# Order of transposes and values in the hand-ordered prompt attention of a hybrid decoder step

## The chip, the cores and the metric

One Trainium2 chip, one core. The metric is the device time of one execution in microseconds (us); the kernel before was run three times, and the median is 2159.5 us.

## The reference, cut to what matters

The reference is one layer of a hybrid decoder for 1024 prompt tokens and 32 sample tokens: an input projection, a gated MLP mixer, an attention with three branches, a merge, and a squared-ReLU MLP. The change touches only the attention of the prompt. There are 8 query heads of width 64 in 2 key/value groups, and for every block of 128 queries and every head three softmaxes are taken, weighted by gates and added:

```
p_c = masked_softmax(einsum(qn, kc) * scale, m_c)      # compressed keys, 64 rows
o_c = einsum(p_c, vc)
p_s = masked_softmax(einsum(qr, k_s) * scale, m_s)     # selected blocks; for 1024 tokens: all causal keys
o_s = einsum(p_s, v_s)
p_w = masked_softmax(einsum(qr, k_w) * scale, m_w)     # sliding window of 512 keys
o_w = einsum(p_w, v_w)
o   = g0 * o_c + g1 * o_s + g2 * o_w
```

## The kernel before, in words

The work runs in stages on one core: projections of the first columns, their values and queries, then the attention of the prompt, the attention of the sample tokens, the merge, and the MLP. All matrix products are made of float32 halves (a rounded part and a rest), so most products come as two or three matmuls.

**The attention of the prompt** (lines 687 to 1046). A unit is one block of 128 queries and one pair of heads; there are 8 times 4 = 32 units (`pairs`, line 689). The keys of a unit, for both heads and all three branches, are laid out as runs of 128 columns, four runs to a chunk (line 722); a unit has 2 to 7 chunks, 160 chunks in all. One step of the stage handles one chunk. What is issued for a chunk c of unit u:

- **Queries**, once a unit: `q_trans` (line 698) takes a PSUM bank "PT" (there are 2), transposes four 128x128 pieces on TensorE, copies them on ScalarE (the rounded half) and subtracts on VectorE (the rest) into `QT` (2 buffers), and then calls `q_load` (line 691), which issues the two DMAs of the queries two units on, on the SP queue, into `qdl` (2 buffers).
- **Logits**: `step(c)` (line 805) takes a PSUM bank "S" (3 of them) and a buffer `P` (8), multiplies `QT` with `KT` (and `KTC` for the compressed keys), takes the masked maximum on VectorE (lines 777 and 779), and, when the last chunk of a head's branch is there, the exponentials on ScalarE (line 788). A bank S is free once its exponentials are taken. When the window branch of a head is complete, `fin` (line 791) forms the factor gate / sum on VectorE, and `scale` (line 802) multiplies the P of both branches with it on POOL.
- **Transposes**: `T(c)` (line 843) transposes the P of the chunk into a bank "PT" (line 849), copies it on ScalarE and subtracts on VectorE, both into `PH` (3 buffers).
- **Values**: `PV(c)` (line 855) multiplies `PH` with the values into the bank "O" (one). After the last chunk of a unit, `E` (line 869) takes O out with ScalarE and VectorE, adds on POOL, and writes it to DRAM from the POOL queue.

Two other pieces of work are spread between the steps: `f0`, the gate columns of the input projection (`fill`, line 884: bank "G", 72 portions of 12 matmuls 128x352), and `comp`, the compression of the sample's cache (line 970: bank "F", 64 portions, of which each second pair holds 12 matmuls 128x256). `comp` also issues the page loads `raw` on the SP queue (line 942, 16 DMAs a set).

**What sets the order.** The stage runs in a manual schedule for TensorE and SP (line 1009): these two execute exactly in the order of the program. ScalarE, VectorE and POOL are not in it: their order is set by the planner, which orders by program position and its own estimates, with some pieces marked as high priority. The order within a step s is lines 1020 to 1043; `LAG` is 6:

```
PV of chunk s-7, and E if it was a unit's last
logits of chunk s
portions of comp and f0
q_trans of the next unit, if chunk s is a unit's first
T of chunk s-6
```

So a chunk's transposes stand last in a step, and its values first in the next.

Of the kernel before, what the change touches and what calls it, by code (L numbers as in the profile page):

```python
# [36 lines left out]
LAG = 6  # L37
# [8 lines left out]
def build(tc, a):  # L46
# [3 lines left out]
    def f(x):  # L50
        return x.bitcast(F32)

    def cp(out, in_, scale=1.0):
        return ACT.activation(out, in_, AF.Copy, scale=scale)  # L54
# [7 lines left out]
    def sub(out, x, y):  # L62
        return tt(out, x, y, OP.subtract)
# [150 lines left out]
    def bank(tag, bufs, p=None):  # L214
        return (p or psS).tile([128, 512], F32, name=tag, bufs=bufs)
# [475 lines left out]
    def q_load(i):  # L691
        if i < len(pairs):
            qb, pr = pairs[i]
            qd_t[i] = p2.tile([128, 4, 2, 64], F32, name="qdl", bufs=2)
            for d in range(2):
                SP.dma_start(qd_t[i][:, :, d], qd_d[qb, :, pr * 256:(pr + 1) * 256].rearrange("p (a d) -> p a d", d=64))

    def q_trans(i):
        if i >= len(pairs):
            return  # L700
        src = qd_t.pop(i).rearrange("p a b d -> p a (b d)")
        pt = bank("PT", 2, psS).rearrange("p (a t) -> p a t", a=4)
        for j in range(4):
            PE.transpose(pt[:, j], src[:, j], ident)
        q = p2.tile([128, 2, 4, 128], F32R, name="QT", bufs=2)
        cp(q[:, 0], pt)
        sub(q[:, 1], pt, f(q[:, 0]))
        qt_t[i] = q
        q_load(i + 2)
# [304 lines left out]
    A, C, steps = {}, {}, []  # L1014
# [3 lines left out]
    nc_ = nf_ = 0  # L1018
    total = len(steps) + LAG
    for s_ in range(total + 1):  # L1020
        if s_ > LAG:
            u, c, last = steps[s_ - LAG - 1]
            C[u][1](c)
            if last:
                C.pop(u)[2]()
        if s_ < len(steps):
            u, c, last = steps[s_]
            if c == 0:
                chunks, Ps, A[u] = a_steps(u)
                assert len(chunks) == sum(x[0] == u for x in steps)  # L1030
                C[u] = c_steps(u, chunks, Ps)
            A[u][c]()
        while nc_ * total < 64 * s_:
            next(comp, None)
            nc_ += 1
        while nf_ * total < 6 * NF0 * s_:
            next(f0, None)
            nf_ += 1
        if s_ < len(steps) and steps[s_][1] == 0:
            q_trans(steps[s_][0] + 1)  # L1040
        if LAG <= s_ < total:
            u, c, last = steps[s_ - LAG]
            C[u][0](c)
    for g in (f0, comp):
        for _ in g:
            pass
# [504 lines left out]
```

## Time and profile before

| | us |
|---|---|
| median of 3 runs | 2159.5 |
| lowest, highest | 2155.89, 2166.57 |
| the profiled execution | 2157.89 |
| its span in the trace | 2156.1 |
| busy in the span: TensorE matmul, VectorE, ScalarE, POOL | 1842.8, 969.1, 717.6, 428.7 |
| first transposes of queries, last values of the prompt (start) | 229.1, 1037.0 |

The profile of one execution gives, for each instruction, its start and its duration. The span is the time from the first to the last instruction of the trace; the profiled execution took 1.8 us more than its span. "PE" is TensorE's matmul, "PEld" its weight load, "DVE" VectorE, "ACT" ScalarE, "SP" the queue that issues most DMAs. A busy TensorE is not TensorE at its peak: consecutive matmuls overlap, and the length of one depends on the clock that was granted.

### The profile page before, as it was taken

The numbers are of one execution on the slowest core, as the hardware profiler recorded it, in microseconds if no ns is written. First come the engines' busy times: TensorE is split into PE (matmuls) and PEld (weight loads), VectorE is DVE, ScalarE is ACT, GpSimd is POOL, SyncE is SP. The second block draws the span as 40 slices with busy tenths as digits, with TensorE's granted clock in tenths as the row PEclk, the third lists the DMA queues.
The fourth block names the chain that finished last, engine by engine and source line by source line (L and its number), as shares of the span: only waits on it lengthen the run. The fifth ranks groups of instructions, "written<-read, shape, count | busy, mean of one in ns | idle before, by whom it ended". The sixth has DMA issues, their size and how long they took to land.

```text
span 2156.1 us, 30189 instructions
## 1 busy us (share of the span) xinstructions
PE 1842.8 (85%) x11071; PEld 1715.0 (80%) x11071; DVE 969.1 (45%) x2374; ACT 717.6 (33%) x1684; POOL 428.7 (20%) x636
## 2 busy tenths in 40 slices
PE   8999567666666666666799899999999999999999
PEld 7878566655666665655566799999999999999999
DVE  7557455444544444443414664453333323333333
ACT  5435354444544444343223422332012102201210
POOL 3113344333333333333212000300000000000000
PEclk9999788889988899898899999999999999999999
DMA  5323422111221111201567443311111111111121
GB/s 170 123 53 115 144 67 61 45 51 54 73 60 40 54 45 53 65 10 45 185 200 220 147 159 100 100 43 49 50 40 50 42 47 50 40 50 50 40 80 61
DMA packets 154118, 168.70 MB, mean 78 GB/s; under 512 B 51825, under 2 KB 128242, under 8 KB 153970
## 3 DMA queue, kind: packets, MB, share of 16 engines
q1 hardware_dynamic: 135586, 133.67, 20.1%
q0 software_dynamic: 7488, 22.29, 3.0%
q10 hardware_dynamic: 10896, 10.82, 1.6%
q8 instruction: 87, 1.43, 0.3%
q14 instruction: 61, 0.50, 0.1%
HBM read 136.54 MB, written 29.13 MB: 77 GB/s over the span
## 4 chain that ended last, share of the span: by engine, by line
PE 76%; DVE 9%; ACT 8%; issue 3%; SPq 2%; DMA 2%; POOL 0%; ACTq 0%; DVEq 0%; POOLq 0%
PE S L73 25%; PE G L73 17%; PE PT L73 12%; PE O L73 11%; PE F L73 9%; DVE PH L57 4%; ACT PH L54 3%; PE PT L849 2%; ACT P L788 2%; SPq L942 1%; ACT hl L54 1%; DMA ol<-o_d 1%; DVE S L779 1%; DVE QT L57 1%; SPq L934 1%
## 5 line engine op out<-in xcount | busy, mean ns | idle before, releaser
L73 PE MATMUL G<-big,whl 128*128 128x352 f32 x1440 | 291.3, 358 | 6.1 <-DVE zu L57 4.5
L73 PE MATMUL O<-PH,V 128*128 128x256 f32 x528 | 105.8, 324 | 222.4 <-DVE PH L57 222.4
L73 PEld LDWEIGHTS G<-big,whl 128*128 128x128 f32 x1440 | 267.2, 216 | 35.0 <-issue 16.5
L73 PEld LDWEIGHTS O<-PH,V 128*128 128x128 f32 x528 | 76.4, 202 | 256.2 <-DVE PH L57 256.0
L54 ACT ACTIVATE whl<-wraw 128x1024 fp32r<-128x1024 f32 x100 | 106.1, 1061 | 436.2 <-PE S L73 145.4
L73 PE MATMUL S<-U,whl 128*128 128x352 f32 x864 | 201.1, 324 | 0.0
L73 PE MATMUL S<-H,whl 128*128 128x352 f32 x840 | 189.9, 324 | 0.0
L803 POOL TENSOR_SCALAR P<-P,rs 128x128 f32<-128x128 f32 (+4 forms) x272 | 130.1, 491 | 203.6 <-DVE rs L57 125.8
L73 PE MATMUL PT<-U,whl 128*128 128x352 f32 x576 | 154.5, 324 | 0.0
L73 PEld LDWEIGHTS S<-U,whl 128*128 128x128 f32 x864 | 149.9, 188 | 0.0
L73 PEld LDWEIGHTS S<-H,whl 128*128 128x128 f32 x840 | 144.7, 188 | 0.0
L73 PE MATMUL PT<-H,whl 128*128 128x352 f32 x528 | 142.8, 324 | 0.0
L54 ACT ACTIVATE PH<-PT 128x512 fp32r<-128x512 f32 (+2 forms) x160 | 86.5, 541 | 155.4 <-PE PT L849 152.8
L779 DVE CUSTOM_DVE_ANT_0 S<-S,mask 128x256 f32<-128x256 f32 (+3 forms) x160 | 77.1, 482 | 131.1 <-PE S L73 126.5
L788 ACT ACTIVATE P<-S,nm 128x512 f32<-128x512 f32 (+3 forms) x208 | 108.4, 528 | 77.3 <-DVE nm L57 48.1
L57 DVE TENSOR_TENSOR PH<-PT,PH 128x512 fp32r<-128x512 f32 (+2 forms) x160 | 99.6, 623 | 73.2 <-ACT PH L54 70.5
L73 PE MATMUL S<-wt,big 128*128 128x512 f32 x408 | 107.3, 411 | 10.6 <-ACT wt L54 6.6
L120 DVE TENSOR_TENSOR whl<-wraw,whl 128x1024 fp32r<-128x1024 f32 x80 | 97.7, 1221 | 14.6 <-ACT whl L54 14.6
L73 PEld LDWEIGHTS PT<-U,whl 128*128 128x128 f32 x576 | 103.2, 188 | 0.0
L73 PE MATMUL S<-KT,QT 128*128 128x128 f32 (+3 forms) x416 | 100.5, 355 | 1.6 <-ACT QT L54 0.8
L73 PE MATMUL F<-H,whl 128*128 128x352 f32 x312 | 101.0, 324 | 0.0
L73 PEld LDWEIGHTS S<-wt,big 128*128 128x128 f32 x408 | 78.4, 197 | 28.2 <-ACT wt L54 6.6
(376 smaller groups left out, 3832.0 us busy)
## 6 DMA issues: line engine op xcount, KB each, us to landing
wraw<-wfm SPq DMA_DIRECT2D x80, 512.0 KB, 3.3
ring<-cs SPq DMA_DIRECT2D x128, 128.0 KB, 2.1
wraw<-wfm POOLq DMA_DIRECT2D x20, 512.0 KB, 3.8
tg<-th_d SPq DMA_DIRECT2D x48, 176.0 KB, 2.8
qdl<-qd_d SPq DMA_DIRECT2D x64, 128.0 KB, 2.4
raw<-cck SPq DMA_DIRECT2D x128, 64.0 KB, 1.9
raw<-ccv SPq DMA_DIRECT2D x128, 64.0 KB, 1.9
wtr<-wtok SPq DMA_DIRECT2D x24, 256.0 KB, 2.9
```

What stands on the lines that cost most here:

```text
L54: return ACT.activation(out, in_, AF.Copy, scale=scale)
L57: return DVE.tensor_tensor(out, x, y, op=op)
L73: return PE.matmul(out, l, r, start=start, stop=stop, skip_group_check=skip)
L120: (POOL if i < FM_BR else DVE).tensor_tensor(t[:, 1], raw, f(t[:, 0]), op=OP.subtract)
L779: DVE.tensor_tensor_reduce(S, S, m, scale=-1.0, scalar=3e38, op0=OP.add, op1=OP.min, accum_out=dst)
L788: ACT.activation(Ps[c][:, lo:hi], Ss[c][:, lo:hi], AF.Exp, bias=nm[:, 0, k:k + 1], scale=todo[h, br, i], accum_out=sm[:, i, k:k + 1])
L803: POOL.tensor_scalar(P, P, rs[:, 1, k:k + 1], 1.0, op0=OP.mult, op1=OP.mult)
L849: PE.transpose(pt[:, j], Ps[c][:, j * 128:(j + 1) * 128], ident)
L934: _, vals = nc.values_load_multi_w_load_instructions(ptab[0:1, i0:i0 + 16], engines=[mybir.EngineType.SP], min_val=0, max_val=159, skip_ru ...
L942: SP.dma_start(dst, src)
```

## The change

The three pieces of a step are put in another order. The transposes T of chunk s-6 go from the end of step s to its beginning, the values PV of chunk s-7 (and E) from the beginning of step s to its end, so that a whole step with its logits and fillers, and the transposes of the following chunk, lie between a chunk's transposes and its values. The queries of the next unit are transposed at the beginning of the last step of the unit before it, no longer at the end of that unit's first step.

```
     for s_ in range(total + 1):
-        if s_ > LAG:
-            u, c, last = steps[s_ - LAG - 1]
-            C[u][1](c)
-            if last:
-                C.pop(u)[2]()
+        if s_ + 1 < len(steps) and steps[s_ + 1][1] == 0:
+            q_trans(steps[s_ + 1][0])
+        if LAG <= s_ < total:
+            u, c, last = steps[s_ - LAG]
+            C[u][0](c)
         if s_ < len(steps):
             u, c, last = steps[s_]
...
         while nf_ * total < 6 * NF0 * s_:
             next(f0, None)
             nf_ += 1
-        if s_ < len(steps) and steps[s_][1] == 0:
-            q_trans(steps[s_][0] + 1)
-        if LAG <= s_ < total:
-            u, c, last = steps[s_ - LAG]
-            C[u][0](c)
+        if s_ > LAG:
+            u, c, last = steps[s_ - LAG - 1]
+            C[u][1](c)
+            if last:
+                C.pop(u)[2]()
```

`C[u][0]` is T, `C[u][1]` is PV, `C[u][2]` is E.

## Rows read from the trace of the kernel before

**Rows 1.** The page: busy time in the whole span, and the span in 40 equal slices of 54 us (busy share in tenths; PEclk is the granted clock in tenths of full speed).

```profile
PE 1842.8 (85%) x11071; PEld 1715.0 (80%) x11071; DVE 969.1 (45%) x2374; ACT 717.6 (33%) x1684; POOL 428.7 (20%) x636
PE   8999567666666666666799899999999999999999
DVE  7557455444544444443414664453333323333333
ACT  5435354444544444343223422332012102201210
POOL 3113344333333333333212000300000000000000
PEclk9999788889988899898899999999999999999999
```

**Rows 2.** Busy time by stretches of the span. Columns: from and to (us), length, busy us (and instructions) of PE, PEld, DVE, ACT, POOL, the granted clock, the share of the DMA engines, GB/s. The first row is the attention of the prompt; the others are stretches inside and outside of it.

```profile
229.00:1038.00 809.00, 533.24 (x3138) 481.05 (x3136) 380.53 (x1217) 355.60 (x1015) 299.37 (x504) 0.88 0.20 57
...
300.00:400.00 100.00, 68.64 (x396) 63.19 (x396) 50.49 (x175) 47.69 (x148) 42.67 (x76) 0.84 0.22 62
...
500.00:600.00 100.00, 67.29 (x416) 60.41 (x416) 49.16 (x156) 46.51 (x129) 41.87 (x66) 0.93 0.20 61
```

**Rows 3.** The same view for stretches of 54 us outside of that stage, where TensorE is busier.

```profile
54.00:108.00 54.00, 54.00 (x299) 46.87 (x298) 31.00 (x104) 26.88 (x50) 7.05 (x7) 1.00 0.39 123
108.00:162.00 54.00, 49.45 (x249) 41.27 (x248) 29.90 (x74) 21.38 (x46) 10.48 (x12) 0.94 0.20 53
...
1188.00:1242.00 54.00, 47.41 (x284) 43.44 (x285) 35.04 (x81) 22.52 (x49) 4.32 (x8) 0.94 0.50 153
```

**Rows 4.** Who waited for whom, TensorE alone, from 229 to 1038 us: the waiting engine, tile and line, what it waited for, us in total, times, longest us. These are all the rows of that answer above 1.1 us.

```profile
PE O L73 <- DVE PH L57: 251.5, 159, 3.6
PE F L73 <- ACT hl L54: 21.1, 1, 21.1
```

**Rows 5.** The timeline of steps around 730 us: start, us, engine, line, operation, tiles, count, and in brackets the idle time of the engine before it and what ended it. Rows of other work are left out.

```profile
722.90 0.69 PE L73 MATMUL S<-KT,QT 128*128 128x384 f32 x4
...
725.40 0.60 PE L849 MATMUL PT<-ident,P 128*128 128x128 f32 x4
...
726.43 0.17 DVE L57 TENSOR_TENSOR rs<-rs,sgate 128x2 f32<-128x2 f32 x1
...
726.80 2.16 POOL L803 TENSOR_SCALAR P<-P,rs 128x512 f32<-128x512 f32 x4 [5.23 <-ACT PH L54]
...
727.47 0.74 PE L73 MATMUL O<-PH,V 128*128 128x256 f32 x4 [1.47 <-DVE PH L57]
...
728.05 0.63 PE L73 MATMUL S<-KT,QT 128*128 128x512 f32 x2
...
728.52 0.60 PE L849 MATMUL PT<-ident,P 128*128 128x128 f32 x4
...
729.16 0.60 ACT L54 ACTIVATE PH<-PT 128x512 fp32r<-128x512 f32 x1 [2.08 <-PE PT L849]
...
729.79 0.69 DVE L57 TENSOR_TENSOR PH<-PT,PH 128x512 fp32r<-128x512 f32 x1 [0.18 <-ACT PH L54]
730.53 0.54 PEld L73 LDWEIGHTS O<-PH,V 128*128 128x128 f32 x4 [1.65 <-DVE PH L57]
730.53 0.74 PE L73 MATMUL O<-PH,V 128*128 128x256 f32 x4 [1.41 <-DVE PH L57]
```

**Rows 6.** The same timeline, the step after it: VectorE's maxima and ScalarE's exponentials of one chunk, and the copy of the next PH behind them on ScalarE.

```profile
731.11 0.74 PE L73 MATMUL S<-KT,QT 128*128 128x128 f32 x4
...
731.89 0.30 DVE L779 CUSTOM_DVE_ANT_0 S<-S,mask 128x128 f32<-128x128 f32 x1 [1.41 <-PE S L73]
...
732.77 0.15 DVE L57 TENSOR_TENSOR nm<-nm 128x1 f32<-128x1 f32 x1
732.96 0.37 ACT L788 ACTIVATE P<-S,nm 128x128 f32<-128x128 f32 x1 [3.20 <-DVE nm L57]
...
734.23 0.20 ACT L788 ACTIVATION_READ_ACCUMULATOR P<-S,nm 128x1 f32 x1
734.32 0.60 ACT L54 ACTIVATE PH<-PT 128x512 fp32r<-128x512 f32 x1
734.95 0.69 DVE L57 TENSOR_TENSOR PH<-PT,PH 128x512 fp32r<-128x512 f32 x1 [2.03 <-ACT PH L54]
```

**Rows 7.** The timeline from 651 to 657 us: the end of a unit (O taken out) and the queries of another.

```profile
651.43 0.38 ACT L54 ACTIVATE o_t<-O 128x256 f32<-128x256 f32 x1
...
652.19 0.42 DVE L57 TENSOR_TENSOR o_t<-O,o_t 128x256 f32<-128x256 f32 x1
...
654.53 0.60 PE L704 MATMUL PT<-ident,qdl 128*128 128x128 f32 x4
...
655.37 0.58 ACT L54 ACTIVATE QT<-PT 128x512 fp32r<-128x512 f32 x1
...
656.11 0.68 DVE L57 TENSOR_TENSOR QT<-PT,QT 128x512 fp32r<-128x512 f32 x1
```

**Rows 8.** The page: DMA issues of the SP queue (KB each, median us from issue to landing), and the timeline row of 15 page loads issued one after the other.

```profile
qdl<-qd_d SPq DMA_DIRECT2D x64, 128.0 KB, 2.4
raw<-cck SPq DMA_DIRECT2D x128, 64.0 KB, 1.9
```

```profile
719.78 8.52 SPq L942 DMA_DIRECT2D raw<-ccv  x15
```

## The prediction, made before the change was run

> **What bounds the kernel now.** I began with the slices of the page [rows 1]: TensorE is at nine tenths or more in most of the span, but from the fifth slice to the nineteenth it shows five to seven tenths, with VectorE, ScalarE and POOL at two to six. That is the attention of the prompt, the only stage that the change touches. The busy times by stretches [rows 2] give its size: 809.0 us, of which TensorE is busy 533.2, VectorE 380.5, ScalarE 355.6, POOL 299.4. No engine is full, so the stage is bound by waits. The waits of TensorE name them [rows 4]: 251.5 us in 159 waits, of the values' matmuls for VectorE's part of PH, and one of 21.1 us, for the first pages of the compression. 533.2 + 251.5 + 21.1 = 805.8 of 809.0: besides these two, TensorE, which follows the program's order, waits for next to nothing. The timeline shows one such wait [rows 5]: transposes at 728.52 for 0.60 us, ScalarE's copy at 729.16 for 0.60, VectorE's subtraction at 729.79 for 0.69, values at 730.53, with TensorE idle for 1.41 us. 251.5 / 159 = 1.58 us a chunk: the bare length of this chain and a little queueing. It is on the path in full, because the values stand directly behind the transposes, and what is behind the values waits too.
>
> **The change, part by part.** *Values a step later.* Between a chunk's transposes and its values there will be, on TensorE, the logits, the fillers, the values of the chunk before, the next step's transposes, logits and fillers. In the step at 727.47 [rows 5], which has no filler, values, logits and transposes take 0.58 + 0.47 + 0.60 = 1.65 us; even two steps without filler put 0.47 + 0.58 + 0.60 + 0.47 = 2.1 us between a chunk's transposes and its values, for a chain of 1.41. The wait goes: **-251.5 us**. The cover is the steps themselves; where ScalarE or VectorE has other work queued ahead of the copies for more than about 0.7 us, part of it is back.
>
> *Buffers.* Two PH are alive at a time where three exist, and P's buffer is read two steps before it is written again where eight exist; both cost nothing. PT: the transposes of a chunk need the bank of two uses before, a full step back. O: a unit's last values and the next unit's first are still one step apart; taking O out lasts 0.38 + 0.42 us [rows 7], against some 1.2 us of transposes and logits. Nothing to 0.8 us at 32 units; I take 0.4 each, **+13**, nearer the middle since both engines have queues.
>
> *Queries.* q_trans moves from a unit's first step to the beginning of the last, so its chain (0.58 on ScalarE, 0.68 on VectorE from transposes at 654.53 to about 656.8, so 1.7 us behind their end [rows 7]) now has one step instead of two to seven in front of the new unit's logits. Without filler that step covers 0.60 + 0.47 + 0.58 + 0.60 = 2.25 us. Nothing to 1 us, 32 times; I take 0.5: **+16**. Its two DMAs move with it on SP: the load two units on is issued at the unit's last step and wanted at least four steps later, and lands in 2.4 us [rows 8]. Page loads that stood behind it now stand ahead of it: 15 of them hold SP for 8.5 us [rows 8], under three steps, so the cost is nothing; if a set of pages came in two-step units it could show as a wait of a few us, four times at most. On POOL nothing is passed but E's DMA, which nobody in the stage waits for.
>
> *Logits closer behind each other.* Now the logits of two chunks are separated by transposes, the 1.4 us wait, and values; the wait disappears. There are three S banks, and the bank is free only after the exponentials: in [rows 6] logits from 731.11, maxima from 731.89, exponentials from 732.96 to 734.43, thus 3.3 us. A group of columns often ends one chunk on, so the logits three chunks on have about two steps for this chain. Before, no wait for S appears in TensorE's list. Bounds: nothing, where a filler stands in these steps; and 0.65 us a step without one, if a copy and a subtraction of PH (0.60 and 0.69 [rows 6]) lie ahead of the chain each time: (3.3 + 1.3) / 2 = 2.3 us a step, where TensorE needs 1.65. Of 166 steps 72 hold a portion of f0 and 32 a heavy one of comp; spread evenly, 166 x 0.57 x 0.81, about 76, hold neither. I take 0.5 us in these: **+38**, nearer the upper end, since the chain of [rows 6] had nothing in its way and was 3.3 us all the same.
>
> *The clock.* TensorE's granted clock is 0.88 over the stage, 0.84 to 0.93 in stretches with two thirds busy [rows 2], and 0.94 to 1.00 where it is busy 47 to 54 us of 54 [rows 3]; it has two levels, 1.2 and 2.4 GHz. With the gaps closed I take 0.95: 533.2 x 0.88 / 0.95 = 494, **-39**. The bounds are no gain (533) and the full clock, 533.2 x 0.88 = 469, so -64. The Trainium skill's page "TensorE: Matmul & The Clock Gate" (Part 1) says that throttled is the default and sustained activity releases it; by that rule the sum would have the full clock and 25 us more of gain, and the rows at 0.94 with TensorE at nine tenths make me stop short of it.
>
> *The sum.* -251.5 - 39 + 13 + 16 + 38 = -223.5, rounded to -220 for the drain at both ends of the stage. The stage goes from 809 to about 589 us. Against the profiled execution's own 2157.9 us that is 1938; the median of the runs, 2159.5, lies 1.6 above it, which I don't carry. The later stages are not touched.
>
> **The rivals.** *VectorE and ScalarE take over as the pace.* They are in order, now hold copies, maxima, exponentials and fillers' evacuations at two thirds of the time, and the planner orders them by estimates. If all 166 steps lose the 0.65 us (108), because the fillers' own copies lie in the same two queues, and O and queries cost 13 + 16, then 137 of the 251.5 come back, with no gain of the clock: 2157.9 - 115 = 2043. For it: the chain of [rows 6] is twice as long as a light step; against: 380 us of VectorE's work in a stage of 590 is 64%.
>
> *Nothing waits.* At the full clock with no more than 25 us of new waits: 469 + 21 + 25 = 515, so 2157.9 - 294 = 1864. For it: the waits list shows nothing behind the removed one. Against: three S banks.
>
> *Slower: the transposes hold the logits.* T stands now at the head of a step, and P must have been scaled. Where a head's window ends in its fourth chunk, its first chunk is scaled from the logits of step 3 on, and transposed at the beginning of step 6: two steps and a rest. A late scaling would stop TensorE before the logits on which the next scaling depends. In [rows 5] logits at 722.90, the factor at 726.43, scaling from 726.80, the first of four pieces done at about 727.5: 4.6 us, while the rest of step 3 and two steps make at least 6 even without fillers. To come out slower than 2157.9 by over 0.5%, 64 heads' first transposes would have to wait (251.5 + 11) / 64 = 4.1 us each, so the chain would have to reach some 13 us, as with POOL behind by several of its long subtractions every time; the time would then be 2169 or more. The same page of the Trainium skill (Part 2, Step-by-step) states that matmuls stay in program order; the trace agrees in that nothing of [rows 5] passes the waiting values, and it is this rule that would make such a wait a full stop.
>
> *It does not do what it says.* If the planner put ScalarE's and VectorE's copies late, next to the values, the wait would stay: 2150 to 2165.
>
> **How the numbers follow.** The forecast (1895 to 1990) has a chance of 0.63, the pace of the other engines (1990 to 2050) 0.19, nothing waits (1850 to 1895) 0.12, the planner 0.03, slower 0.03. Three runs of the kernel lie within 0.5% of each other (2155.9 to 2166.6), about what a measurement of it can tell from no change. So faster by over 0.5%: 0.94; within: 0.03; slower: 0.03. The range leaves out about a third of the side cases and the two small ones: 1870 to 2025.
>
> **What would show it.** TensorE's waits for PH under 40 us in all; the stage at 550 to 630 us; the granted clock there at 0.93 or more; TensorE's busy time in it below 510; new waits for S, QT or O, together 40 to 100 us, none for POOL's scaling over 20. The prediction is wrong if PH still leads the waits, if TensorE waits over 150 us for S banks or P, or if its busy time in the stage does not fall while the waits go.

## The result, and the profile after

The changed kernel takes 1867.7 us (median of 4 runs, 1863.56 to 1870.18) against 2157.7 before: a ratio of 0.865, interval 0.8616 to 0.8684. The forecast was 1938 with a range of 1870 to 2025. The direction held, and so did the main mechanism, the wait for PH; the gain was 290 us and not 220, which puts the time just outside the range. The profiled execution took 1865.99, its span is 1864.2.

The page of the changed kernel, whole span and 40 slices of 46.6 us; it answers to [rows 1]:

```profile
PE 1755.0 (94%) x11071; PEld 1656.1 (89%) x11071; DVE 937.6 (50%) x2374; ACT 708.9 (38%) x1684; POOL 429.6 (23%) x636
...
PE   8999958899899987889999999999999999999999
...
DVE  7647747767777675413665445333333333333332
ACT  5534447777777665222422333310231023102310
POOL 3112447666556565212100220000000000000000
PEclk9999969999999999899999999999999999999999
```

The attention of the prompt is now slices six to sixteen, with TensorE at eight or nine tenths in all but the first of them (five tenths: it holds the wait for the first pages) and the last (seven). TensorE's instructions are the same 11071, but its busy time fell by 88 us. The stretches of the stage from its first transposes to its last values, first of the changed kernel, then of the one before, with the same columns as [rows 2]:

```profile
230.10:737.60 507.50, 440.87 (x3116) 420.71 (x3115) 346.61 (x1203) 344.20 (x1000) 300.82 (x503) 0.96 0.31 89
```

```profile
229.10:1037.30 808.20, 532.68 (x3136) 480.71 (x3134) 379.73 (x1216) 355.12 (x1014) 298.84 (x503) 0.88 0.19 57
```

The stage went from 808.2 to 507.5 us, by 300.7. TensorE's idle time in it (length less busy) went from 275.5 to 66.6, by 208.9, and its busy time from 532.7 to 440.9, by 91.8. The rest of the span rose by 8.8 us (1347.9 to 1356.7). The waits of TensorE in the changed kernel, which answer to [rows 4]:

```profile
PE F L73 <- ACT hl L54: 21.4, 1, 21.4
PE O L73 <- DVE o_t L57: 12.9, 13, 1.8
PE F L73 <- DVE ch_g L454: 8.0, 5, 2.9
PE PT L849 <- DVE QT L57: 7.1, 11, 1.4
PE F L73 <- DVE pcs L1123: 5.1, 1, 5.1
PE PT L849 <- DVE PH L57: 4.6, 5, 1.8
...
PE O L73 <- DVE PH L57: 2.9, 2, 2.0
...
PE S L73 <- ACT P L788: 1.9, 2, 1.3
...
PE PT L849 <- POOL P L803: 0.7, 1, 0.7
```

The wait of the values for PH, 251.5 us in 159 pieces, is 2.9 in two. Nothing took its place at its size. A timeline of two steps shows why, to be held against [rows 5] (rows of other work left out):

```profile
513.58 0.60 PE L849 MATMUL PT<-ident,P 128*128 128x128 f32 x4
...
513.93 0.77 PE L73 MATMUL S<-KT,QT 128*128 128x384 f32 x4
...
514.22 0.60 ACT L54 ACTIVATE PH<-PT 128x512 fp32r<-128x512 f32 x1 [0.51 <-PE PT L849]
...
514.54 2.13 PE L73 MATMUL G<-big,whl 128*128 128x352 f32 x12
...
515.23 0.69 DVE L57 TENSOR_TENSOR PH<-PT,PH 128x512 fp32r<-128x512 f32 x1
...
516.51 0.64 PE L73 MATMUL O<-PH,V 128*128 128x256 f32 x4
...
516.99 0.60 PE L849 MATMUL PT<-ident,P 128*128 128x128 f32 x4
...
518.03 0.72 PE L73 MATMUL O<-PH,V 128*128 128x256 f32 x4
```

The PH begun by the transposes at 513.58 is ready at 515.92 (515.23 + 0.69) and used at 518.03; VectorE could have been 2 us later without TensorE noticing. And the transposes, 0.60 us long in both traces, are followed by the logits 0.35 us after their start: the last one's end overlaps with what follows. In [rows 5] nothing followed it, and the 0.60 counted in full as busy time.

### The profile page after: what moved, and what is told of

Read it like the earlier page. It is cut to its first block, busy times and chain, and to the rows that moved or that the text cites. A ratio compares the mean times of both kernels' runs of the same rounds, so it can differ in the third digit from the quotient of the medians.

```text
span 1864.2 us, 30205 instructions
## 1 busy us (share of the span) xinstructions
PE 1755.0 (94%) x11071; PEld 1656.1 (89%) x11071; DVE 937.6 (50%) x2374; ACT 708.9 (38%) x1684; POOL 429.6 (23%) x636
## 4 chain that ended last, share of the span: by engine, by line
PE 57%; SPq 2%; DVE 1%; DMA 1%; issue 1%; ACT 1%; POOL 0%; ACTq 0%; DVEq 0%
PE S L73 20%; PE PT L73 12%; PE G L73 11%; PE O L73 7%; PE F L73 7%; SPq L942 1%; DMA ol<-o_d 1%; SPq L934 1%; DMA ring<-cs 0%; PE PT L849 0%; DVE rkB L57 0%; DVE rkA L57 0%; DVE zu L57 0%; ACT qp L54 0%; PE PT L1239 0%
## 5 line engine op out<-in xcount | busy, mean ns | idle before, releaser
L73 PE MATMUL G<-big,whl 128*128 128x352 f32 x1440 | 267.4, 336 | 8.8 <-DVE zu L57 3.9
L73 PEld LDWEIGHTS G<-big,whl 128*128 128x128 f32 x1440 | 240.1, 195 | 38.7 <-issue 18.8
L73 PE MATMUL O<-PH,V 128*128 128x256 f32 x528 | 89.5, 291 | 15.8 <-DVE o_t L57 12.9
L849 PE MATMUL PT<-ident,P 128*128 128x128 f32 x560 | 89.1, 275 | 13.5 <-DVE QT L57 7.1
```

The costliest lines, as they stand in the source:

```text
L73: return PE.matmul(out, l, r, start=start, stop=stop, skip_group_check=skip)
L849: PE.transpose(pt[:, j], Ps[c][:, j * 128:(j + 1) * 128], ident)
```

## The experiments

Twelve kernels were run. "Before" is about 2157 us throughout, the changed kernel 1867.7. Diffs are against the changed kernel unless the old order is named.

**Parts of the change**

*e1_queries_only*, in the old order:

```
     for s_ in range(total + 1):
+        if s_ + 1 < len(steps) and steps[s_ + 1][1] == 0:
+            q_trans(steps[s_ + 1][0])
         if s_ > LAG:
...
-        if s_ < len(steps) and steps[s_][1] == 0:
-            q_trans(steps[s_][0] + 1)
```

> The kernel before with one part of the change alone: the queries of the next unit are transposed at the beginning of the last step of a unit. Values stay directly behind their transposes. Theory (the gain is the distance between a chunk's transposes and its values, and what that distance does to TensorE's clock and restarts): the wait for PH stays at about 250 us, time 2150 to 2165. Rival (the place of the queries frees the logits or the PT banks and has a share in the gain): PH wait lower by 20 us or more, time under 2140.

Measured: 2120.8 us, ratio 0.983 (0.9802 to 0.9851), so faster by 35; the stage of its trace is 36.6 us shorter.

```profile
PE O L73 <- DVE PH L57: 233.4, 158, 3.3
...
230.00:1001.60 771.60, 514.07 (x3135) 462.69 (x3133) 377.71 (x1216) 354.72 (x1014) 298.41 (x504) 0.90 0.20 59
```

PH's wait is down 18 where 20 was asked of the rival; the time is under 2140. In substance the rival holds: in the old order the place of the queries had a price. The timeline of TensorE in the old trace, in a unit's first step, and below it that of this kernel, in a unit's last step:

```profile
654.53 0.60 PE L704 MATMUL PT<-ident,qdl 128*128 128x128 f32 x4
654.97 0.60 PE L849 MATMUL PT<-ident,P 128*128 128x128 f32 x4
657.89 0.74 PE L73 MATMUL O<-PH,V 128*128 128x256 f32 x4 [2.32 <-DVE PH L57]
```

```profile
648.16 0.60 PE L849 MATMUL PT<-ident,P 128*128 128x128 f32 x4
648.59 0.60 PE L704 MATMUL PT<-ident,qdl 128*128 128x128 f32 x4
650.25 0.74 PE L73 MATMUL O<-PH,V 128*128 128x256 f32 x4 [1.05 <-DVE PH L57]
```

In the old order the queries stood directly ahead of the chunk's transposes, so their copy and subtraction stood ahead of PH's in both queues. The 2.32 us is one of the longer cases: over the 28 such steps of the old trace the wait was 1.82 us in the mean, against 1.55 in the other 128. In this kernel the queries stand between a chunk's transposes and its values, so that their copies come behind PH's and their own matmuls fill a part of the wait: it is 1.22 us in the mean of those 28 steps. The two effects make 17 of the 18 us. The other half of the 36.6 us is TensorE's busy time (532.7 to 514.1, with the granted clock at 0.90).

*e2_queries_old*:

```
-        if s_ + 1 < len(steps) and steps[s_ + 1][1] == 0:
-            q_trans(steps[s_ + 1][0])
...
+        if s_ < len(steps) and steps[s_][1] == 0:
+            q_trans(steps[s_][0] + 1)
         if s_ > LAG:
             u, c, last = steps[s_ - LAG - 1]
```

> The changed kernel with the queries put back to the end of a unit's first step; transposes first and values at the end of the next step are kept. Theory: the whole gain is there, 1855 to 1880; the 7 us that transposes wait for the bank of the queries go or move. Rival (the place of the queries has a share): over 1885.

Measured: 1873.9 us, 0.869 (0.8671 to 0.8712), 6 us above the changed kernel, with overlapping intervals. The wait of the transposes for the bank of the queries falls from 7.1 to 1.1 us, and others of a few us come. With a step's distance the place of the queries no longer matters to speak of: the two parts act on the same wait.

*e3_same_step*:

```
-        if s_ > LAG:
-            u, c, last = steps[s_ - LAG - 1]
+        if LAG <= s_ < total:
+            u, c, last = steps[s_ - LAG]
             C[u][1](c)
```

> The changed kernel with the values of a chunk at the end of the same step in which it is transposed first, not of the next: between them stand only the logits and the step's fillers. Theory: in the some 76 steps without a filler the logits (0.47 us) cover only a part of the 1.41 us chain, about 0.95 us each is back, plus queueing: PH waits 70 to 110 us, time 1940 to 1985, and the granted clock of the stage falls to about 0.93. Rival (any work between is enough, the fillers hide it): PH waits under 30 us, 1870 to 1890.

Measured: 1959.4 us, 0.909 (0.9069 to 0.9107).

```profile
PE O L73 <- DVE PH L57: 113.1, 82, 3.5
...
229.00:834.60 605.60, 465.36 (x3118) 434.49 (x3118) 354.50 (x1201) 349.48 (x1008) 298.75 (x503) 0.94 0.26 76
```

The time is as the theory had it, the wait a little above. It isn't only the steps without a filler: TensorE stops ahead of the values in 58 steps that hold logits alone (83 us in all), but also in 28 with a portion of filler (28 us), which doesn't always cover the chain. The second step of distance is worth 92 us.

**Is the fall of the busy time the clock?**

*e4_idle_filled*, in the old order:

```
             ph = phs.pop(c)
+            for i in range(10):
+                mm(O[:, i % 2], zw, KT[:, 0, 0:256], c == 0 and i == 0, False, True)
...
-                    mm(O[:, h], v.rearrange("p a d -> p (a d)"), ph[:, :, j], c == 0 and j == 0, False, True)
+                    mm(O[:, h], v.rearrange("p a d -> p (a d)"), ph[:, :, j], False, False, True)
```

> The kernel before, in its old order, with ten matmuls of 256 columns by a tile of zeros in front of each chunk's values, into the same bank O: they need nothing of PH and fill the time in which TensorE waited (about 1.3 us at full clock against a wait of 1.58). They add zeros, so nothing of the result is left out. Theory (about 60 us of the fall of TensorE's busy time is the clock, which sank because TensorE idled): the granted clock of the stage rises to 0.96 or more, the fillers' matmuls into G fall from 373 ns to about 335, the wait for PH is under 60 us, and the time is 2070 to 2120 although no wait was shortened and 1600 matmuls are added. Rival (busy time fell because matmuls behind a stop pay a restart, and the clock has no part): G stays at 365 ns or more, time 2150 or above.

Measured: 2104.3 us, 0.976 (0.9735 to 0.9776): 1600 matmuls more, and 52 us less. The stage of this kernel, and its fillers into G (busy us, mean ns of one); then the same group before and after the change:

```profile
229.00:986.60 757.60, 657.18 (x4735) 616.16 (x4732) 379.93 (x1209) 354.69 (x1012) 299.15 (x502) 0.97 0.21 61
...
L74 PE MATMUL G<-big,whl 128*128 128x352 f32 x864 | 156.4, 331 | 0.0
```

```profile
L73 PE MATMUL G<-big,whl 128*128 128x352 f32 x864 | 185.1, 373 | 0.0
```

```profile
L73 PE MATMUL G<-big,whl 128*128 128x352 f32 x864 | 158.3, 333 | 2.2 <-POOL whl L120 2.2
```

The fillers run as fast with the wait filled as with the wait gone, 331 and 333 ns against 373; the granted clock is 0.97. PH's wait is somewhat over what was expected:

```profile
PE O L74 <- DVE PH L58: 73.2, 126, 2.6
```

The stage is 808.2 - 757.6 = 51 us shorter with the chain still on the path. This is what the clock gave back, less what the ten matmuls cost where they outlasted the wait: 126 waits of 159 are left, so in some 33 chunks they did.

The clock's part can also be read from the traces by itself, because the granted clock is recorded stretch by stretch, each at one of two levels (1.00 and 0.50 of full speed, 2.4 and 1.2 GHz). These are the sums over the stage's stretches at 0.50 (us, and busy us of the engines), before and after the change, and twelve matmuls into G in the old trace, at the full level and almost wholly at the lower:

```profile
sum 201.38, PE 160.85 PEld 152.22 DVE 80.83 ACT 71.82 POOL 83.73; mean PE 4.35 PEld 4.11 DVE 2.18 ACT 1.94 POOL 2.26
```

```profile
sum 44.37, PE 22.93 PEld 22.21 DVE 13.95 ACT 15.92 POOL 19.39; mean PE 4.59 PEld 4.44 DVE 2.79 ACT 3.18 POOL 3.88
```

```profile
685.87 2.07 PE L73 MATMUL G<-big,whl 128*128 128x352 f32 x12
...
710.11 3.65 PE L73 MATMUL G<-big,whl 128*128 128x352 f32 x12
```

At the lower level the same work takes 3.65 us and not 2.07, so 1 - 2.07 / 3.65 = 0.43 of the busy time there is what the clock costs. TensorE was busy 160.9 us at that level before and 22.9 after: the clock's part is 0.43 x 138, by this estimate about 60 us.

*g3_old_sub_twice*, in the old order; *g1_new_sub_twice* has the same edit in the new one:

```
             sub(ph[:, 1, 0:n], pt[:, 0:n], f(ph[:, 0, 0:n]))
+            sub(ph[:, 1, 0:n], pt[:, 0:n], f(ph[:, 0, 0:n]))
```

> The kernel before with VectorE's subtraction of each PH made twice. There the chain is on TensorE's path: theory, the wait for PH grows by the whole 0.62 to 0.69 us at each of 160 chunks, to about 350 us, and the clock sinks further: time 2255 to 2285. Rival (a part of the wait is queueing that absorbs it): under 2230.

Measured: 2383.9 us, 1.103 (1.0997 to 1.1062): 225 us slower for 98 us of work, far more than either side expected. Waits of TensorE and the stage:

```profile
PE O L73 <- DVE PH L57: 319.9, 135, 4.4
...
PE O L73 <- DVE sm L57: 19.5, 9, 2.3
PE O L73 <- DVE rs L57: 14.0, 6, 2.6
PE O L73 <- DVE rs L799: 10.5, 4, 3.2
...
PE O L73 <- ACT P L788: 3.5, 2, 1.9
...
229.00:1268.00 1039.00, 643.18 (x3147) 585.40 (x3147) 475.35 (x1381) 355.76 (x1018) 300.60 (x503) 0.73 0.15 44
```

The waits in front of O (those on sm, rs and P are the same wait, with another instruction named as the last) grew to some 367 us, by 116, about what was expected. The rest is TensorE's own work: 643 us busy, 110 more, for the same instructions at a granted clock of 0.73. TensorE is busy 418.6 us at the lower level here, 258 more than before; 0.43 of that is 111.

**How much room do the other engines have?**

> The changed kernel with VectorE's subtraction of each PH made twice (the second writes the same values): 160 times 0.62 us, 98 us more of VectorE's work in a stage of 508 us, and a chain 0.69 us longer between transposes and values. Theory (TensorE is the bound of the stage and the others have room: VectorE is busy 347 of 508): VectorE rises to about 0.85, small waits grow, time 1870 to 1910. Rival (VectorE paces the stage already, and TensorE only follows): the whole 98 us, 1950 or more.

Measured: 1903.3 us, 0.881 (0.8796 to 0.8826): 36 us for 98 us of work. VectorE is busy 430.5 us of a stage of 549:

```profile
229.00:778.00 549.00, 458.77 (x3123) 432.60 (x3121) 430.50 (x1363) 348.31 (x1007) 300.48 (x505) 0.93 0.30 85
```

*g2_new_copy_twice*:

```
             cp(ph[:, 0, 0:n], pt[:, 0:n])
+            cp(ph[:, 0, 0:n], pt[:, 0:n])
```

> The same with ScalarE's copy of each PH made twice: 160 times 0.54 us, 87 us more of ScalarE's work. Theory (room): time 1870 to 1905. Rival (ScalarE paces): 1940 or more.

Measured: 1887.1 us, 0.874 (0.8699 to 0.878): 19 us for 87. Both within the theory of room: the same edit that costs 225 us in the old order costs 36 in the new. The room isn't free, though: about a third of VectorE's added work and a fifth of ScalarE's comes out.

**Where would the transposes hold the logits?**

*f1_lag4*, *f4_lag5*, *g4_lag7*: one line, `LAG = 6` to 4, 5 and 7.

> The changed kernel with LAG 4 in place of 6: a chunk is transposed four steps after its logits. Where a head's window branch ends in the unit's fourth chunk, the first chunk's P is scaled in step 3 and transposed at the beginning of step 4. Theory (it is the two steps of room between scaling and transposes that keep the transposes at a step's head from holding the logits; a step is now some 3.1 us and the chain from the logits to the scaled P 4.6 us): TensorE waits for POOL's scaling, 2 to 4 us for each head of the largest units and less elsewhere, in all 20 to 80 us; time 1885 to 1945. Rival (the scaling is never late, the room has no part): under 1880.

> The changed kernel with LAG 5 in place of 6. Theory of the room: one whole step and a rest are about 4 to 5 us against a chain of 4.6, so the wait for the scaling is small, 3 to 20 us, and the time 1868 to 1890. Rival (no part): 1860 to 1872 and no such wait.

> The changed kernel with LAG 7 in place of 6, one step more of room between scaling and transposes. Theory (with LAG 6 TensorE waits 0.7 us for the scaling in all, nothing is left to win): 1860 to 1875. Rival (what is left of TensorE's waits, 46 us without the first pages, comes from the tight distance): under 1850.

Measured: LAG 4 1921.5 us (0.892, 0.8895 to 0.894), LAG 5 1879.8 (0.871, 0.8697 to 0.8731), LAG 7 1865.7 (0.864, 0.862 to 0.8657). The wait of the transposes for POOL's scaling, LAG 4 first, then LAG 5:

```profile
PE PT L849 <- POOL P L803: 40.7, 22, 3.6
```

```profile
PE PT L849 <- POOL P L803: 10.3, 11, 3.0
```

With LAG 6 it is 0.7 us. This is the mechanism of the rival that ended slower, and where it sets in: the kernel loses 54 us at LAG 4 and 12 at LAG 5, of which the wait itself is 40.7 and 10.3, and the wait is next to nothing at 6. LAG 7 can't be told from 6; what is left of the waits does not come from this distance.

**An attempt at a faster version**

*f2_comp_later*:

```
-        while nc_ * total < 64 * s_:
+        if s_ == 4:
+            cl.q.append(cl.fns.pop(0)())
+        while nc_ * (total - 8) < 64 * (s_ - 8):
```

> The changed kernel with the sample's compression begun eight steps later (its 64 portions spread over the 158 steps left) and its first set of pages requested in step 4. It aims at the 21.4 us for which TensorE waits for the first pages in both kernels, before and changed. Theory (that wait is on the path in full, since nothing else bounds these steps): it falls under 5 us, time 1845 to 1858. Rival (the stage is paced by VectorE and ScalarE after all, which then have the same work in less time, or the pages stand in front of the queries' loads on SP): 1860 to 1870.

*f3_comp_later_evac_first* adds `with tc.high_priority():` around `cp(t1, ...)` and `add(t1, ...)` in E.

> The kernel of the run before, and besides, the two operations that take O out at a unit's end (ScalarE's copy, VectorE's addition) are given high priority in the planner's order. In the changed kernel TensorE waits 12.9 us in 13 waits for that addition. Theory (the wait comes from the order in the two queues): the wait falls under 5 us and the time by another 5 to 10, to 1837 to 1852. Rival (the two operations are early enough in the queues, what is ahead of them is only moved behind and is late next): no difference from the run before, within 4 us.

Measured: 1873.8 us (0.867, 0.8639 to 0.8691) and 1870.8 (0.867, 0.8657 to 0.8689); no gain from either. f2 lies outside both of its ranges, the rival's too; f3 differs from f2 by 3 us, as its rival said. Waits and the stage of f2:

```profile
PE G L73 <- ACT whl L54: 12.8, 2, 11.6
...
PE O L73 <- DVE o_t L57: 5.0, 8, 1.4
...
PE F L73 <- ACT hl L54: 1.5, 1, 1.5
...
228.00:745.40 517.40, 453.24 (x3114) 432.41 (x3113) 357.43 (x1203) 343.86 (x1000) 297.46 (x502) 0.94 0.31 88
```

The 21.4 us for the first pages are gone, as meant, but the first weights of the gate columns, which had been hidden behind that wait, are late in their turn by 11.6. TensorE's idle time in the stage is 64.2 us against 66.6, so the theory that the wait was on the path in full falls: something was waiting just behind it. The busy time rose by 12 us; TensorE is busy 46.7 us at the lower level here against 22.9, which makes 10 of it the clock's by the estimate above. In f3 the wait for O is 5.9 us, no lower than in f2 (5.0), so the priority shows no effect; that it is under 12.9 in both was not explained. No version tried beats the changed kernel by more than the intervals.

## Why the prediction was wrong

| term | forecast, us | measured, us | from |
|---|---|---|---|
| wait for PH | -251.5 | -244.0 | 2.9 + 4.6 left |
| TensorE's busy time ("the clock") | -39 | -91.8 | 532.7 to 440.9 |
| O | +13 | +12.9 | wait for o_t |
| queries | +16 | +7.1 | wait of the transposes for QT's bank |
| S banks | +38 | +1.9 | wait of the logits for P |
| other new waits in the stage | 0 | +13.2 | remainder, 8.0 of it for ch_g |
| rest of the span | 0 | +8.8 | 1347.9 to 1356.7 |

The measured terms add up to -291.9 us, the difference of the two spans.

**The step that failed is "The clock".** It priced TensorE's work at 533.2 x 0.88 / 0.95 = 494 us and called 469 its lower bound; it is 441. Three things make up the 53 us:

- The clock came out at 0.96 and not 0.95: 489 by the same formula, 5 us.
- The mean clock of a stage is no price for its work, because it counts the time in which TensorE idles. Before, TensorE was busy in 161 of the 201 us at the lower level, 80%, but in 372 of the other 607, 61%. The estimate of 60 us for the clock (e4 above) leaves 473: 16 us more than the formula gives.
- The other 32 us are, by this estimate, not the clock, and for them the prediction had no term. A stop costs TensorE busy time as well: the ends of the last transposes overlap with nothing when nothing follows them (0.60 us in front of a stop, 0.35 to the logits in the new order), and four matmuls of values show 0.74 us behind a stop (730.53 in [rows 5]) and 0.64 without one (516.51).

The runs bear out this division. Where the stops stayed, the clock's estimate gives the change of busy time alone: 17 of 18.6 us in e1 (busy 120.7 us at the lower level), 111 of 110.5 in g3. Where stops went, a rest is left: 32 us for the 157 waits for PH that are gone in the changed kernel, and in e3 (busy 52.7 us at the lower level; the estimate is 47 of 67.3) 20 us for 77. That is 0.20 and 0.26 us a stop. How the rest divides between the ends of the transposes and the first matmuls behind a stop was not tried. The Trainium skill's page "Perfetto Trace Analysis" (Tensor Engine Instruction) says that the end of a matmul is estimated by the profiler and not observed; the 0.60 that stands in both traces whatever follows agrees.

**S banks** was next, 36 us too dear. The chain of [rows 6] was taken as it stood in the old trace, 3.3 us, and laid against two steps without filler in a row, half the time. The wait is 1.9 us in two pieces. A likely reason, not tried by itself, is that the steps are mixed: over the stage one takes 507.5 / 166 = 3.1 us, and two of them hold the chain with nearly 3 us left. The rival of the other engines as the pace falls by g1 and g2.

**Queries** was priced only as a loss of cover, a wait of the new unit's logits for QT. That wait is the same 1.6 us in both kernels, at the first unit alone; the 7.1 us are transposes that wait for the bank "PT" until VectorE's part of QT is done. In the old order the move alone is a gain, 35 us in e1, of which the wait of 2.32 us at 657.89 was a sign. In the changed kernel that gain is inside the wait for PH, so it is not counted twice.

**Right**: that the chain of 1.41 us was on the path in full and that a step and its fillers cover it (PH's waits 7.5 us where under 40 was said), nothing lost in SP's order, and the scaling of P with room for its two steps, which LAG 4 and 5 bear out. **Right by luck**: O, where 0.4 us at each of 32 units was said and 13 waits of 1.0 us in the mean came. **Wrong, and small**: "PT" was to cost nothing, but the transposes wait for that bank, 7.1 us behind QT and 4.6 behind PH. **Not foreseen**: the rest of the span. In the old trace the sample's first scores ran before the last values of the prompt; now they stand behind the stage, with TensorE idle 5.1 us for pcs. But a wait of 5.9 us for s_new that the old trace has there is gone: over the first 112 us behind the stage TensorE waits 16.5 us and waited 13.4. The rest of the 8.8 us was not traced.

The nearest case of the prediction was the rival in which nothing waits, 1864 us, with a chance of 0.12. That it came within 2 us of the profiled execution's 1866 is luck: it allowed 25 us of waits besides the one for the pages where there are 45 (66.6 - 21.4), and held TensorE's work at 469 where it is 441.

## What to carry to other kernels

A stop of TensorE in each of many short steps cost more here than its idle time: 92 us beside 244. Price the clock by the busy time at each level and not by the mean clock of the stage, and price the overlap that the matmuls around a stop get back. Put the producer of a cross-engine chain first in a step and its consumer at the end of the next. With one step of distance the short steps decide (e3: 113 us of waits); with two, nearly every chain was covered. When an operation is moved out of the way of such a chain, look whose copies it stood ahead of, and which wait it now fills: its move can gain, too.

## What was not expected of the hardware

The same 0.62 us of VectorE's work a chunk cost 225 us in one order and 36 in the other; half of the 225 is TensorE's clock, which went from 0.88 to 0.73 in the stage as the stops grew. Over the whole stage the granted clock is 0.73, 0.88, 0.90, 0.94, 0.96 and 0.97 with TensorE busy 62, 66, 67, 77, 87 and 87% of it (g3, before, e1, e3, changed, e4): it fell as TensorE was kept less busy and rose as it was kept busier. The Trainium skill's page "TensorE: Matmul & The Clock Gate" (Part 1) says that throttled is the default and activity releases it; the order of these six stages agrees. The busy share alone does not give the clock, though: the two shorter stretches of [rows 2], both inside the stage, show 0.84 and 0.93 with TensorE busy 69 and 67%. And matmuls with nothing but zeros, in the time in which TensorE would have stopped, made a kernel 52 us faster.
